# Spectra operands made four products ahead, stored spectra requested by ScalarE, another order of units

## The chip, the cores and the metric

The kernel runs on one core of one Trainium2 chip. A core has five engines with queues of their own: TensorE (matmuls; PE in the rows, its weight loads PEld), VectorE (DVE), ScalarE (ACT), GpSimd (POOL) and SyncE (SP), which here only requests transfers. Sixteen DMA engines move data between the main memory and the on-chip memory; requests to them come from the queues of SyncE, GpSimd and ScalarE. The metric is the device time in microseconds of one execution. Before the change it is 2862.4 us, the median of three runs (2861.56 to 2863.65).

## The reference, cut to what matters

The reference computes two layers of a diffusion backbone over 1024 latent tokens and 256 context tokens of width 1024. The change touches the first layer alone, and there the Hyena half of the mixer: two long convolutions, each with a filter that a small network makes, applied in the frequency domain.

```python
def long_conv(u, filt, skip):
    L = u.shape[1]
    uf = jnp.fft.rfft(u, n=2 * L, axis=1)
    ff = jnp.fft.rfft(filt, n=2 * L, axis=0)
    y = jnp.fft.irfft(uf * ff[None], n=2 * L, axis=1)[:, :L]
    return y + u * skip

def hyena_mix(p, conv_w, conv_b, w1, b1, freq, w2, b2, w3, skip):
    ...
    v = x1 * long_conv(v, filt[:, 0], skip[0])
    v = x2 * long_conv(v, filt[:, 1], skip[1])
    return v.astype(p.dtype)
```

Around it stand the input projection, a Fourier mixer on the other half of the channels, the output projection, a gated feed-forward block, and a second layer with neighbourhood attention.

## The kernel before, in words

All products run in fp32r, an fp32 format of reduced precision. Each operand is therefore split into a high part, rounded by ScalarE (line 350), and a low part, the difference, subtracted by VectorE (line 352). A product is then three matmuls: high by high, high by low, low by high. All matmuls of the transforms are written by one helper (line 346), all requests of SyncE by another (line 331, `ld`), those of ScalarE by a third (`lda`, line 334) and those of GpSimd by a fourth (`ldr`, line 337), so that rows of the profile show these lines.

The Fourier transforms are matmuls with stored cosine and sine matrices, folded by symmetry. A frequency belongs to a class: even or odd index (`cls` 0 or 1), and cosine or sine (`eo`).

**Spectra of the filters.** `spectrum_l(o, ...)` makes the spectrum of the filter of convolution `o` (0 or 1) for the latent tokens while the input projection runs; both are woven together by generators, in a list that says how many steps of the filter work follow each block of the projection. For each class in the order 2, 3, 0, 1 it takes four operands, each a sum or difference of filter rows in a high and a low part, with a stored matrix: sixteen operands in all. Two operands (`k` = 0, 1) share a group of twelve matmuls, into two accumulators (`f` = 0, 1). The inner generator `operands()` makes them: it loads a pair of matrices (`cast2`, two `tk` tiles out of a pool of four, requested by GpSimd, which rounds while it moves), forms the sums on VectorE (`sums`, lines 958 to 975, and lines 998 to 1002), and splits them. For class 0 it first forms `f0` (lines 982 to 984), and the first group of that class also makes the highest frequency, with products whose output has two rows (128*2 in the rows). The list `ready` holds the operands that are made before they are used; each product takes one out and asks for another. The spectra are stored in main memory by SyncE, a pair of 128 by 512 blocks for each class and block of frequencies.

**The units.** After the projection, `unit(o, fb, cls)` computes one block `fb` of 128 frequencies of class `cls` of the transformed input, and multiplies it with the stored spectrum. It requests its matrices (16 bit, rounded by ScalarE at lines 399 and 414; or through GpSimd, where `wide` is set), requests the stored spectrum `F` (an `s4` tile of 128 by 1024, 512 KB, from a pool of 21), and runs its matmuls in two halves: a class 0 unit has 6 matmuls in each half, a class 1 unit 12. The first half needs the input rows of even index, the second those of odd index. Then `combine_l` forms the complex product: two wide VectorE multiplications (lines 1256 and 1257), two additions on GpSimd (line 1261 and the next), and, one unit later, the split in `parts()` (ScalarE line 1273, VectorE line 1275). The split result keeps two `s4` tiles until the inverse has used it. Eight units make a convolution, so sixteen of the 21 tiles then hold results.

**Between the two convolutions.** `inverse_first` computes the inverse of the first convolution and the gate `x1`, in two passes `j` = 0, 1; each pass gives half of the rows that the second convolution transforms (even ones in the first pass). In the last pass it starts the first halves of four units of the second convolution, so that TensorE has work while VectorE makes the odd rows; the fourth of them uses the two `pq` accumulators, the others the six `ps` ones. Afterwards each unit is finished and the unit four places later started. `inverse_last` (line 1425) follows, with the Fourier mixer of the latent tokens woven in.

**What sets the order.** The program text gives each instruction a priority by its place. A planner, part of the framework, then plays the program through with costs of its own, and fixes for each engine an order, by what is ready and has a free buffer in its play, earliest in the text first. On the chip each queue keeps that order. So a generator step that is taken earlier raises the priority of its instructions, and a load waits for its buffer at the head of the queue that requests it.

Of the kernel before, what the change touches and what calls it, by code (L numbers as in the profile page):

```python
# [258 lines left out]
class Builder:  # L259
# [685 lines left out]
    def spectrum_l(self, o, raw, tot):  # L945
# [32 lines left out]
        def operands():  # L978
            for i in classes:
                if i == 0:  # L980
                    f0 = self.f0 = self.S2()
                    V.tensor_copy(f0, fe)
                    V.tensor_tensor(f0[0:1, :], fe[0:1, :], fo[0:1, :], ADD)
                    V.scalar_tensor_tensor(f0[0:1, :], f0[0:1, :], 0.5, self.taps0[o][0:1, :], op0=MUL, op1=ADD)
                even = []
                for p in (0, 1):
                    with self.follow(self.row_ld):
                        mt = self.cast2(a["ff_l"][i, p])
                    for k in (0, 1):
                        if i % 2 == 0:  # L990
                            if p == 0:
                                even.append(sums(i, k))
                            t = even[k][p]
                        else:
                            f, r = (raw[(p + 2 * k, q, i // 2)] for q in (0, 1))
                            t = self.T()
                            if i == 1 and p + k == 0:
                                V.scalar_tensor_tensor(t, r, m1, f0, op0=MUL, op1=ADD)
                            elif p + k == 0:
                                V.scalar_tensor_tensor(t, f, m0, r, op0=MUL, op1=ADD)  # L1000
                            else:
                                V.tensor_tensor(t, f, r, SUB if i == 1 else ADD)
                        xh, xl = self.S2(F32R), self.S2(F32R)
                        self.split(t, xh, xl)
                        yield xh, xl, mt[k]

        ops = operands()
        ready = [next(ops), next(ops)]
        yield
        for i in classes:  # L1010
            cls, eo = i % 2, i // 2
            kept = []
            for p in (0, 1):
# [22 lines left out]
                for f in (0, 1):  # L1036
                    fb = 2 * p + f
                    if eo:
                        self.frg[("l", o, cls, fb)] = self.DR([2, P, HC])
                    d = self.frg[("l", o, cls, fb)]  # L1040
# [276 lines left out]
    def unit(self, o, fb, cls, bank=None, wide=False):  # L1317

        a = self.a
        tr = self.tr  # L1320
        if cls == 0:
            src = a["vfe_l"][fb]
            mt = self.cast4(src) if wide else self.cast(1024, src) if o + fb == 0 else self.cmat(1024, src)
            mats = [mt[:, :512], mt[:, 512:]]
            q = 2 * (fb // 2)
            xs = [range(q, q + 2), range(4 + q, 6 + q)]
        else:
            src = a["vfo_l"][fb]
            half = [src[:, j * 1024:j * 1024 + 1024] for j in (0, 1)]
            mats = [self.cast4(x) for x in half] if wide else [self.cast(1024, x) for x in half] if o + fb == 0 else self.cmat2(src)  # L1330
            xs = [range(4, 8), range(4)]
        F = self.S4()
        d = self.frg[("l", o, cls, fb)]
        self.ld(F.rearrange("p (e c) -> p e c", e=2), d[0:2].rearrange("e p c -> p e c"))
        row = None
        if cls == 0 and fb == 0:
            row = self.TK()
            self.ld(row[0:1, :], self.frow[("l", o)])
        bank = bank or self.PS
        spec = [bank(), bank()]  # L1340
        n = len(xs[0])
        H = n * P
        for half in (0, 1):
            for ps, mt, x in zip(spec, mats, xs):
                for b in range(half, n, 2):
                    sl, sk = slice(b * P, (b + 1) * P), slice(H + b * P, H + (b + 1) * P)
                    xh, xl = tr[x[b]]
                    self.mm(ps, mt[:, sl], xh, b == 0, False)
                    self.mm(ps, mt[:, sl], xl, False, False)
                    self.mm(ps, mt[:, sk], xh, False, b == n - 1)  # L1350
            yield
        self.combine_l(o, cls, fb, spec, F, row)
        yield
# [1177 lines left out]
    def run(self):  # L2531
# [78 lines left out]
        for k, (fb, cls) in enumerate(((0, 1), (0, 0), (1, 1), (1, 0), (2, 1), (3, 1), (2, 0), (3, 0))):  # L2610
# [5 lines left out]
            if k in (0, 1, 6):  # L2616
                next(cc)
        self.parts()
        units = [self.unit(1, fb, cls, self.PQ if k % 4 == 3 else None, k in (2, 3))
                 for k, (fb, cls) in enumerate(((0, 1), (1, 1), (2, 1), (0, 0), (1, 0), (3, 1), (2, 0), (3, 0)))]  # L2620
        for _ in range(2):
            next(cc)
        for _ in self.inverse_first(units[:4]):
# [136 lines left out]
        for i, _ in enumerate(first_part(1)):  # L2760
            if i == 7:
                c = self.rms_begin(0)
# [54 lines left out]
        c = self.rms_begin(1)  # L2817
# [87 lines left out]
```

## Time and profile before

| | before |
|---|---|
| median of three runs | 2862.4 us |
| profiled execution, its own time | 2867.56 us |
| its span, first to last instruction | 2865.8 us |
| TensorE busy | 2779.7 us, 97% |
| VectorE busy | 2045.2 us, 71% |
| ScalarE busy | 1321.0 us, 46% |
| GpSimd busy | 543.2 us, 19% |
| mean granted clock of TensorE | 0.984 |

The rows in the prediction come from these views. The page gives the totals. The stretches give for each interval its length, then the busy time and number of instructions of TensorE, its weight loads, VectorE, ScalarE and GpSimd, then the clock that TensorE was granted (1.00 is full), the share of the DMA engines in use, and their rate in GB/s. The timeline gives start, duration, engine, line, operation, output and inputs by tile name, shapes and a count; in brackets stands how long the engine was idle before it, and what released it. The waits give engine, line and what was waited for, with the total, the number of times and the longest, in microseconds. Times are counted from the start of the span. Tile names are cut of their numbers: `s` is any tile of the `s2` and `s4` pools, `ps` and `pq` are accumulators, `d` is main memory.

### The profile page before, as it was taken

To read this page: it belongs to the slowest core of one execution; us is meant where nothing else is said; L and a number is where in the kernel's file an instruction comes from. 1 tells how busy PE (TensorE), PEld (TensorE's weight loads), DVE (VectorE), ACT (ScalarE), POOL (GpSimd) and SP (SyncE) were. 2 spreads that over 40 slices of the span, in tenths; PEclk is the share of its full clock that TensorE was granted. 3 is DMA by queue.
4 is the path that set the end of the run, shared out by engine and by line. 5 is a ranking of instruction groups with operands and counts; after the bars stand their busy time and mean duration, and the time that the engine had idled before them with its cause. 6 is when DMAs were issued, how large, how long until landed. Compare 5 with 4: busy or idle time off the path is not lost.

```text
span 2865.8 us, 43630 instructions
## 1 busy us (share of the span) xinstructions
PE 2779.7 (97%) x15610; PEld 2325.6 (81%) x15610; DVE 2045.2 (71%) x3531; ACT 1321.0 (46%) x2269; POOL 543.2 (19%) x880
## 2 busy tenths in 40 slices
PE   7999999999999999999999999999999999999998
PEld 4876678788899888888888888888887788888887
DVE  6766777768777888866777536878867987655556
ACT  5433335443554333333455326888755533333434
POOL 2210234241001211222110002332212122112000
PEclk9999899999999999999999999999999999999999
DMA  7356525655556656658884436777856366434763
GB/s 267 120 167 214 158 83 190 220 172 219 204 189 210 207 192 200 212 196 328 308 308 154 147 120 143 195 203 200 227 199 215 122 242 224 144 110 167 234 195 133
DMA packets 296887, 554.21 MB, mean 193 GB/s; under 512 B 81872, under 2 KB 128658, under 8 KB 296670
## 3 DMA queue, kind: packets, MB, share of 16 engines
q1 hardware_dynamic: 232318, 361.06, 40.0%
q0 software_dynamic: 61504, 185.65, 18.6%
q10 hardware_dynamic: 2848, 4.72, 0.4%
q8 instruction: 123, 2.02, 0.3%
q14 instruction: 94, 0.77, 0.1%
HBM read 405.01 MB, written 118.76 MB: 183 GB/s over the span
## 4 chain that ended last, share of the span: by engine, by line
PE 71%; issue 3%; DVE 3%; DMA 2%; ACT 1%; POOL 1%; DVEq 0%; SPq 0%; POOLq 0%; ACTq 0%
PE ps L1932 25%; PE ps L346 15%; PE ps L2109 11%; PE pq L346 9%; PE pq L1932 3%; PE pq L2109 3%; PE ps L2230 2%; PE ps L2463 1%; PE ps L1425 1%; DMA s<-d 1%; DMA s<-in_c_ctx 1%; DMA g<-in_bias 0%; DMA s<-in_x_t 0%; DVE wl L352 0%; DVE s L352 0%
## 5 line engine op out<-in xcount | busy, mean ns | idle before, releaser
L1932 PE MATMUL ps<-s,s 128*128 128x512 f32 x2012 | 498.6, 391 | 3.3 <-DVE s L1823 1.7
L1932 PEld LDWEIGHTS ps<-s,s 128*128 128x128 f32 x2012 | 379.4, 189 | 83.9 <-DVE s L1823 2.6
L346 PE MATMUL ps<-s,wh 128*128 128x256 f32 (+1 forms) x1776 | 403.3, 331 | 6.0 <-ACT wh L350 2.5
L346 PEld LDWEIGHTS ps<-s,wh 128*128 128x128 f32 x1776 | 296.3, 191 | 41.3 <-ACT wh L350 3.4
L346 PE MATMUL ps<-s,wl 128*128 128x256 f32 (+1 forms) x888 | 267.1, 329 | 0.1
L2109 PE MATMUL ps<-s,s 128*128 128x512 f32 (+1 forms) x1000 | 259.7, 383 | 3.2 <-DVE s L352 3.1
L350 ACT CAST s<-s 128x1024 fp32r<-128x1024 f32 (+2 forms) x192 | 173.0, 926 | 192.0 <-DMA s<-d 172.3
L346 PE MATMUL pq<-s,wh 128*128 128x512 f32 (+1 forms) x848 | 260.9, 389 | 0.3 <-ACT wh L350 0.3
L352 DVE TENSOR_TENSOR wl<-ws,wh 128x1024 fp32r<-128x1024 f32 (+1 forms) x141 | 168.2, 1194 | 118.4 <-ACT wh L350 113.9
L350 ACT CAST wh<-ws 128x1024 fp32r<-128x1024 f32 (+1 forms) x141 | 144.7, 1026 | 204.4 <-PE ps L346 85.4
L346 PE MATMUL ps<-s,s 128*128 128x65 f16 (+4 forms) x2748 | 230.3, 235 | 6.3 <-DVE st L2446 2.6
L352 DVE TENSOR_TENSOR s<-s,s 128x1024 fp32r<-128x1024 f32 (+2 forms) x170 | 191.0, 1154 | 58.3 <-ACT s L350 58.2
L352 DVE TENSOR_TENSOR s<-t,s 128x512 fp32r<-128x512 f32 (+2 forms) x238 | 151.5, 652 | 104.6 <-ACT s L350 81.7
L350 ACT CAST s<-t 128x512 fp32r<-128x512 f32 (+2 forms) x238 | 133.8, 582 | 188.4 <-PE ps L1932 68.0
L2109 PEld LDWEIGHTS ps<-s,s 128*128 128x128 f32 x1000 | 184.4, 188 | 41.2 <-DVE s L352 4.8
L1932 PE MATMUL ps<-s,wh 128*128 128x512 f32 x624 | 194.8, 390 | 0.0
L346 PEld LDWEIGHTS ps<-s,wl 128*128 128x128 f32 x888 | 165.6, 190 | 16.6 <-DVE wl L352 0.6
L337 POOL DMA_DIRECT2D d<-s x186 | 101.4, 546 | 376.5 <-DVE s L1739 92.9
L346 PEld LDWEIGHTS pq<-s,wh 128*128 128x128 f32 x848 | 150.5, 189 | 22.8 <-issue 1.2
L346 PE MATMUL pq<-s,wl 128*128 128x512 f32 (+1 forms) x424 | 161.8, 382 | 1.3 <-DVE wl L352 1.3
L2109 PE MATMUL ps<-s 128*128 128x512 f32 (+1 forms) x500 | 150.7, 385 | 0.0
L346 PEld LDWEIGHTS ps<-s,s 128*128 128x128 f32 (+1 forms) x828 | 129.3, 192 | 22.3 <-issue 4.4
(487 smaller groups left out, 5485.8 us busy)
## 6 DMA issues: line engine op xcount, KB each, us to landing
s<-d SPq DMA_DIRECT2D x282, 256.0 KB, 3.9
d<-s POOLq DMA_DIRECT2D x170, 256.0 KB, 3.7
s<-in_down SPq DMA_DIRECT2D x150, 256.0 KB, 4.1
s<-in_ada_w POOLq DMA_DIRECT2D x64, 512.0 KB, 5.0
ws<-in_up SPq DMA_DIRECT2D x44, 512.0 KB, 3.7
d<-g POOLq DMA_DIRECT2D x86, 256.0 KB, 3.1
ws<-in_gate SPq DMA_DIRECT2D x42, 512.0 KB, 4.3
d<-tk POOLq DMA_DIRECT2D x66, 256.0 KB, 4.0
```

The costliest lines, as they stand in the source:

```text
L337: self.last_ldr = self.nc.gpsimd.dma_start(out, in_).ins
L346: self.last_mm = self.nc.tensor.matmul(o, l, r, start=st, stop=sp).ins
L350: self.last_hi = nc.scalar.copy(hi, src).ins
L352: self.last_lo = eng.tensor_tensor(lo, src, hi.bitcast(F32), SUB).ins
L1425: nc.tensor.matmul(d, s, w, start=cb not in first, stop=e == 1 and i == 1 and f == 3 and k == 2, skip_group_check=True)
L1932: nc.tensor.matmul(ps, x[:, sl], y, start=first and j == 0 and x is wh and y is xh, stop=j == 3 and x is wl, skip_group_check=True)
L2109: m = nc.tensor.matmul(acc[j][:, c0:c1], x[:, sl], y[:, xs], start=first and k == 0, stop=last and k == 2, skip_group_check=True)
L2230: m = nc.tensor.matmul(o, x[:, nb * P:(nb + 1) * P], t[:, c:c + 256], start=kb == 0 and k == 0 and nb % 2 == 0, stop=kb == NFB - 1 and k = ...
L2463: nc.tensor.transpose(ps[:, j * P:(j + 1) * P], src[:, j * P:(j + 1) * P], self.ident)
```

## The change: what it does

It has three parts, at three places.

1. In `spectrum_l`, four operands are made before the first product, where there were two; since each product takes one and asks for one, the generator stays four ahead.
2. In `unit`, the stored spectrum `F` is requested by ScalarE, where SyncE did it. This holds for the sixteen units of both convolutions.
3. In `run`, the units of the second convolution stand in another order. The flags that go with the place stay: the third and fourth unit take their matrices through GpSimd, the fourth and eighth use the `pq` accumulators.

```diff
@@ spectrum_l
         ops = operands()
-        ready = [next(ops), next(ops)]
+        ready = [next(ops) for _ in range(4)]
         yield
@@ unit
         F = self.S4()
         d = self.frg[("l", o, cls, fb)]
-        self.ld(F.rearrange("p (e c) -> p e c", e=2), d[0:2].rearrange("e p c -> p e c"))
+        self.lda(F.rearrange("p (e c) -> p e c", e=2), d[0:2].rearrange("e p c -> p e c"))
         row = None
@@ run
         units = [self.unit(1, fb, cls, self.PQ if k % 4 == 3 else None, k in (2, 3))
-                 for k, (fb, cls) in enumerate(((0, 1), (1, 1), (2, 1), (0, 0), (1, 0), (3, 1), (2, 0), (3, 0)))]
+                 for k, (fb, cls) in enumerate(((0, 0), (0, 1), (1, 0), (1, 1), (2, 1), (3, 1), (2, 0), (3, 0)))]
```

## The prediction

> **What bounds the kernel now.** I read the page first, then the waits of TensorE, then the stretches around its longest waits, and last the order on VectorE, ScalarE and the queues there.
>
> ```profile
> span 2865.8 us, 43630 instructions
> PE 2779.7 (97%) x15610; PEld 2325.6 (81%) x15610; DVE 2045.2 (71%) x3531; ACT 1321.0 (46%) x2269; POOL 543.2 (19%) x880
> PE 71%; issue 3%; DVE 3%; DMA 2%; ACT 1%; POOL 1%; DVEq 0%; SPq 0%; POOLq 0%; ACTq 0%
> ```
>
> TensorE is busy for 97% of the span and carries 71% of the chain of waits. It has 86 us without work (2865.8 − 2779.7), and the change can gain only from its gaps, and from what follows a gap. Four gaps lie where the diff works: two in the stored spectra (about 177 and 297 us), one where the inverse of the first convolution starts (510), one behind the units of the second convolution (568). These are the stretches (length, busy time of each engine with counts, granted clock, share and rate of the DMA engines):
>
> ```profile
> 177.00:193.00 16.00, 13.02 (x33) 7.57 (x32) 8.15 (x15) 2.53 (x5) 0.99 (x2) 0.68 0.41 133
> 297.00:318.00 21.00, 16.43 (x43) 9.92 (x42) 12.30 (x20) 7.46 (x13) 2.34 (x5) 0.67 0.61 199
> 510.30:522.00 11.70, 8.18 (x25) 6.54 (x25) 3.49 (x8) 2.69 (x4) 2.30 (x5) 0.71 0.94 316
> 568.00:590.00 22.00, 17.65 (x97) 14.86 (x97) 18.69 (x17) 9.56 (x11) 19.52 (x13) 0.84 0.39 129
> ```
>
> In each the idle time is only a part of the loss: behind the gap the granted clock is low, 0.67 to 0.84 over the stretch. The same twelve products show it, before the second gap and after it:
>
> ```profile
> 282.96 3.01 PE L346 MATMUL ps<-s,tk 128*128 128x512 f32 x12
> 310.32 5.07 PE L346 MATMUL ps<-s,tk 128*128 128x512 f32 x12
> ```
>
> So I count as lost the idle time plus length times (1 − clock): 2.98 + 5.12 = 8.1 us; 4.57 + 6.93 = 11.5; 3.52 + 3.39 = 6.9; 4.35 + 3.52 = 7.9. That is 34 us in all, and it is the most that the change can bring; where idle time and low clock overlap it is a little less.
>
> **Part 1, four operands ahead in the spectra.** Sixteen operand pairs are made per order, in the classes 2, 3, 0, 1; the gaps stand at the first products of class 0.
>
> ```profile
> 166.82 2.88 PE L346 MATMUL pq<-s,tk 128*128 128x512 f32 x12
> 172.03 0.62 PE L346 MATMUL ps<-s,tk 128*128 128x512 f32 x2
> 180.30 0.40 PE L346 MATMUL ps<-s,c 128*2 128x512 f32 x1 [2.66 <-ACT s L350]
> 288.68 0.63 PE L346 MATMUL pq<-s,tk 128*128 128x512 f32 x2
> 301.99 0.58 PE L346 MATMUL ps<-s,c 128*2 128x512 f32 x1 [3.44 <-ACT s L350]
> ```
>
> TensorE waits there for ScalarE's rounding (line 350), which waits for VectorE, and VectorE is late for one reason: the class 0 operands take seventeen instructions of it, and it began them late.
>
> ```profile
> 167.70 1.30 DVE L352 TENSOR_TENSOR s<-t,s 128x512 fp32r<-128x512 f32 x2 [7.23 <-ACT s L350]
> 168.91 0.48 DVE L982 COPY s<-s 128x512 f32<-128x512 f32 x1
> 180.28 0.69 DVE L352 TENSOR_TENSOR s<-t,s 128x512 fp32r<-128x512 f32 x1
> 283.22 1.29 DVE L352 TENSOR_TENSOR s<-t,s 128x512 fp32r<-128x512 f32 x2 [2.57 <-ACT s L350]
> 284.43 0.42 DVE L982 COPY s<-s 128x512 f32<-128x512 f32 x1
> 301.97 0.69 DVE L352 TENSOR_TENSOR s<-t,s 128x512 fp32r<-128x512 f32 x1
> ```
>
> From the copy at 168.91 to the last subtraction at 180.28 VectorE is busy without a break, some 12 us, after it had stood idle for 7.23 us. The operands are asked for two products earlier under the change. Two products are one group of twelve matmuls: class 3's first group starts at 166.82 and its second at 172.03, so the request moves up by 5.2 us in the first order; in the second order the groups start at 282.96 and 288.68, 5.7 us. Both leads are larger than the waits (2.66 and 3.44), and VectorE has room before (7.23 and 2.57 idle). If the planner keeps the order in which the work is written, both waits close and the low clock behind them goes too: 8.1 + 11.5 = 19.6 us.
>
> What is late next are the stored matrices. A pair of them takes two of the four `tk` buffers, so four operands ahead fill all four, and the loads of the next pair wait for the release whatever the program asks for.
>
> ```profile
> 308.27 0.53 POOL L337 DMA_DIRECT2D tk<-in_ff_l  x1 [11.05 <-PE ps L346]
> tk<-in_ff_l POOLq DMA_DIRECT2D x32, 256.0 KB, 3.2
> 317.54 1.63 PE L346 MATMUL ps<-s,tk 128*128 128x512 f32 x6 [0.79 <-DMA tk<-in_ff_l]
> ```
>
> A load is there 0.53 + 3.2 = 3.7 us after its buffer is free, while the other pair keeps TensorE busy for about 2.7 us (twelve starts within the 3.01 quoted). Where nothing else is on TensorE, that is 1.0 us of waiting per pair, for the two pairs of class 1 in both orders: 4 us given back. The 17 VectorE instructions now compete with the evacuations of the input projection that they used to follow; no row shows that competition, and I bound it by 0 and by the gap that it would reopen, 2.66 us an order, and take 1.3 each, as the idle 7.23 us is nearer to no competition at all. Part 1: 19.6 − 4 − 2.6 = **13 us**; ends 0 and 19.6. Two more pairs of `s2` buffers are held, of 35; no row tells how many are free.
>
> **Part 2, the stored spectra requested by ScalarE.** Sixteen loads of 512 KB leave SyncE's queue.
>
> ```profile
> 502.37 1.23 DVE L1256 TENSOR_TENSOR s<-ps,s 128x1024 f32<-128x1024 f32 x1 [2.90 <-DMA s<-d]
> L1256 DVE TENSOR_TENSOR s<-ps,s 128x1024 f32<-128x1024 f32 x14 | 17.0, 1217 | 12.8 <-DMA s<-d 7.7 <-PE ps L346 5.1
> SPq L331 <- ACT mat L414: 53.7, 11, 13.0
> L334 ACTq DMA_DIRECT2D d<-s x16: 326/326/1144, 1371.8 to 1529.3; - x16
> 450.00:500.00 50.00, 49.22 (x256) 41.65 (x257) 41.15 (x50) 33.18 (x50) 30.04 (x20) 1.00 0.61 201
> ```
>
> Today SyncE stands for 53.7 us behind matrices whose buffers ScalarE still reads, and VectorE waits 7.7 us in all for the spectra queued behind them. The last of these, 2.90 us, is ahead of the third gap. A request of ScalarE took 0.326 us, so sixteen are 5.2 us of its sequencer, and in the 50 us of the first units ScalarE is busy for 33.18 only. TensorE, though, is busy for 49.22 of these 50: what VectorE gains there is hidden, and only the third gap can pay.
>
> ```profile
> 510.78 0.67 DVE L1384 TENSOR_TENSOR t<-tk,ps 128x512 f32<-128x512 f32 x1
> 512.58 1.21 DVE L1275 TENSOR_TENSOR s<-s,s 128x1024 fp32r<-128x1024 f32 x1
> 513.85 22.91 PE L346 MATMUL ps<-s,mat 128*128 128x512 f32 x88 [3.52 <-DVE s L1275]
> ```
>
> The subtraction that ends this gap stands on VectorE behind line 1384, which reads what TensorE itself has just finished. An earlier spectrum moves it only if the planner also puts it ahead of that line. Between 0 and 6.9 us I take **1**, nearer to the row. The Trainium skill (DMA: Bandwidth & Descriptors, Issuing engines are not separate DMA queues) says that requesting from several engines saves only sequencer time, usually small beside the transfer; by it this part would be 0 and the sum 1 us smaller. The trace shows the request itself late, by SyncE's 53.7 us of standing, which the page does not weigh.
>
> **Part 3, the order of the second convolution's units.** The work is the same: four units of 12 matmuls (class 0), four of 24 (class 1), and the same loads. The old first unit is a 24.
>
> ```profile
> 547.21 0.74 PE L346 MATMUL ps<-s,mat 128*128 128x512 f32 x2 [0.94 <-ACT s L350]
> 558.14 11.21 PE L346 MATMUL ps<-s,mat 128*128 128x512 f32 x48 [0.81 <-ACT mat L399]
> 575.56 0.74 PE L1425 MATMUL ps<-mat,s 128*128 128x256 f32 x4 [2.34 <-DVE s L1257]
> 550.64 0.68 DVE L352 TENSOR_TENSOR s<-g,s 128x512 fp32r<-128x512 f32 x1
> 556.46 1.23 DVE L1256 TENSOR_TENSOR s<-ps,s 128x1024 f32<-128x1024 f32 x1 [5.13 <-PE ps L346]
> ```
>
> VectorE ends the transformed rows at 551.3 and then waits 5.13 us for a first finished unit; later TensorE waits for VectorE's combinations (2.34 us and smaller ones, the fourth stretch). With (0, 0) first, a unit needs six matmuls behind rows that are made first of all, so VectorE starts about 5 us earlier, and the combinations behind it with it: 5.0 of the 7.9 us lost. Against it, the first halves started ahead are 6 + 12 + 6 + 12 = 36 matmuls in place of 42; 6 at 0.23 us (11.21 us for 48) uncover 1.4 us near 547, where 0.94 us is open already. Part 3: **3.6 us**; ends −1.4 and 7.9.
>
> The sum is 13 + 1 + 3.6 = 17.6 us. The profiled execution took 2867.56 us with its span of 2865.8; the median shown is 2862.4, 5.2 us lower, and the gaps have no reason to differ, so I take the sum from the median: 2844.8, **2845 us**, own range 2835 to 2852.
>
> **Rivals.** *The matrices take the place.* The waits at class 0 go, but the loads into four `tk` buffers become the rhythm, and each 1.0 us wait brings the low clock back for a group (5.07 − 3.01 = 2.06 us): two pairs in two orders, 4 × 3.06 = 12.2 us given back of 19.6. With part 3 alone beside it the gain is 7.4 + 3.6 = 11: 2851 us. For it speaks the 0.79 us already open; against it, that matmuls of the input projection fill such places elsewhere. The Trainium skill (TensorE: Matmul & The Clock Gate, The HAM clock gate) puts the drop to half rate behind at least one idle window of about 3.4 us; by it waits of 1.0 us would leave the clock alone and this rival would shrink into the forecast. The trace shows a lower clock after a wait of 2.66 us already (0.68 in the first stretch).
>
> *The order does not move.* The operands need `t` buffers (six here) and `s2` buffers as well; if these are what the planner waits for, the class 0 chain begins where it began, part 1 is nothing, and part 3 alone leaves 2859 us. For it speaks that ScalarE's and VectorE's order comes out of the planner, not out of the text; against it, VectorE's 7.23 idle us with ScalarE as releaser, not a buffer.
>
> *ScalarE is held by its requests: slower.* A request waits, in ScalarE's own queue, for a free `s4` buffer; the stored products hold sixteen of 21. Behind it stand the roundings of matrices and products that TensorE needs. ScalarE has 16.8 idle us for the eight requests of the first units (50 − 33.18), 2.1 us each: that is the point from which TensorE pays. At a mean hold of 3.6 us it pays 1.5 × 16 = 24 us, more than the 17.6 gained: 2869 us. For it speaks the tight buffer; against it, that the planner places the request where its model has the buffer free, and that today's requests mostly found their buffer free at once.
>
> **How the numbers follow.** Forecast 0.48, matrices 0.22, order unmoved 0.15, ScalarE held 0.15. About 0.2% (5.7 us) is what can be told from no change. The first two are faster by more, 0.70; the third lies within it, 0.15; the last is slower, 0.15. The range is 2832 (the 34 us nearly whole) to 2868, which takes in the first three and the near end of the fourth.
>
> **What would show it.** Part 1 right: no wait at the 128*2 products of class 0, a granted clock near 1.00 from 177 to 193 and from 297 to 318, class 0's copy (line 982) some 5 us before its place today. Wrong: the same waits, or waits for `tk` loads. Part 2: no VectorE wait for spectra between 457 and 504, and the third gap about as long as now; wrong if ScalarE idles ahead of roundings with a request in its queue. Part 3: VectorE's first combination within 2 us of the last row, and waits below 2 us behind the units. The forecast is wrong as a whole if gaps of this size with their low clock open elsewhere, since a shifted plan can move any later instruction.

## The result, and the profile after

The changed kernel takes 2852.68 us, the median of seven runs (2849.41 to 2857.97), beside 2862.40 us for seven runs of the kernel before (2857.96 to 2864.04). The ratio is 0.9967, 95% interval 0.9956 to 0.9978: 9.4 us gained, with an interval of 6 to 13 us. A later comparison gave 0.9967 again (0.9955 to 0.9978). The forecast was 2845 us, a gain of 17.6.

The profiled execution after took 2850.3 us, 17.3 less than the one before (2867.56). That is nearly twice what the medians differ by: the one before lies 5.2 us above its median, the one after 2.4 below. So a stretch of these two traces may be read for what happens in it, but the gain is read from the medians.

The page of the kernel after, its totals and the DMA queue of ScalarE's requests:

```profile
span 2848.5 us, 43624 instructions
PE 2762.6 (97%) x15610; PEld 2314.2 (81%) x15610; DVE 2044.6 (72%) x3531; ACT 1319.0 (46%) x2269; POOL 543.9 (19%) x880
q10 hardware_dynamic: 7200, 13.11, 1.4%
```

The last line is part 2 at work: that queue moved 13.11 MB, where it moved 4.72 before, and the difference is sixteen spectra of 512 KB.

The first thing to see is where the gain is not. TensorE was idle for 86.1 us before (2865.8 − 2779.7) and is idle for 85.9 us now (2848.5 − 2762.6). The same 15610 matmuls took 17.1 us less busy time. What the change brought is granted clock, not idle time removed.

Every timed run comes with the span and the mean granted clock, so this can be taken over runs. Span times (1 − clock) is an estimate of the time lost to a lowered clock; the rest of the span holds the work at full clock and all idle time. In the two traces it is 45.9 and 28.5 us, 17.4 apart, close to the 17.1 us of busy time. Means, with the standard error of the two parts:

| kernel | runs | span | lost to the clock | the rest |
|---|---|---|---|---|
| before | 79 | 2859.8 | 37.5 (0.5) | 2822.3 (0.3) |
| after | 12 | 2850.5 | 28.0 (0.9) | 2822.4 (0.9) |

The spans differ by 9.3 us; the loss to the clock by 9.5, the rest by nothing.

The stretches show the place. First the kernel before, from the first product of the filter spectra to the last one, then the kernel after, the same work, and two shorter stretches of it (columns as in the prediction):

```profile
143.40:323.20 179.80, 167.84 (x739) 118.88 (x740) 113.11 (x204) 57.64 (x100) 19.62 (x37) 0.91 0.57 187
```

```profile
144.40:314.90 170.50, 158.54 (x748) 114.35 (x749) 113.45 (x204) 56.64 (x100) 19.72 (x37) 0.98 0.61 199
177.00:193.00 16.00, 15.77 (x73) 11.26 (x73) 9.12 (x16) 5.09 (x9) 2.64 (x5) 1.00 0.60 188
297.00:318.00 21.00, 18.54 (x88) 13.88 (x87) 5.09 (x8) 5.40 (x9) 6.04 (x12) 1.00 0.61 180
```

The stretch is 9.3 us shorter. Its idle time is 11.96 us in both (179.80 − 167.84; 170.50 − 158.54). Its clock rose from 0.91 to 0.98: lost time 16.2 us before, 3.4 us after, 12.8 less. That it is not shorter by as much is because nine more matmuls of the projection lie in it (748 against 739), some 2 us, and because the clock is given to a hundredth, 1.8 us of such a stretch. The two places where the prediction saw the gaps, 177 to 193 and 297 to 318, now run at full clock.

The waits did not vanish, they moved. The timeline of the kernel after, TensorE:

```profile
279.42 0.96 PE L346 MATMUL pq<-s,tk 128*128 128x512 f32 x3 [0.45 <-DMA tk<-in_ff_l]
280.79 0.97 PE L346 MATMUL pq<-s,tk 128*128 128x512 f32 x3 [0.40 <-DMA tk<-in_ff_l]
284.96 0.64 PE L346 MATMUL ps<-s,wh 128*128 128x256 f32 x2 [3.21 <-ACT s L1043]
294.65 1.64 PE L346 MATMUL ps<-s,c 128*2 128x512 f32 x6
307.43 1.65 PE L346 MATMUL pq<-s,tk 128*128 128x512 f32 x6 [0.67 <-ACT s L1043]
309.42 1.65 PE L346 MATMUL ps<-s,tk 128*128 128x512 f32 x6 [0.34 <-DMA tk<-in_ff_l]
316.78 0.73 PE L346 MATMUL ps<-s,wh 128*128 128x512 f32 x2 [1.45 <-DVE s L1053]
504.16 1.22 PE L346 MATMUL ps<-s,mat 128*128 128x512 f32 x2 [3.55 <-DVE s L1275]
536.19 0.73 PE L346 MATMUL ps<-s,mat 128*128 128x512 f32 x2 [2.30 <-ACT s L350]
562.71 0.52 PE L1425 MATMUL ps<-mat,s 128*128 128x256 f32 x3
595.07 0.47 PE L346 MATMUL pq<-mat,s 128*128 128x256 f32 x2 [1.05 <-DVE t L1240]
```

The class 0 products with two output rows (128*2) start with no wait, where they waited 3.44 us. In place of that wait stands one of 3.21 us ten microseconds ahead of them: a matmul of the input projection waits for an accumulator, which ScalarE has not yet copied away (line 1043). With the smaller ones of the second order the new waits are 6.5 us (0.45 + 0.40 + 3.21 + 0.67 + 0.34 + 1.45); the three that the prediction showed of the spectra were 6.9 (2.66 + 3.44 + 0.79). ScalarE and VectorE of the kernel after show why:

```profile
283.81 0.62 ACT L350 CAST s<-t 128x512 fp32r<-128x512 f32 x1 [3.65 <-DVE t L970]
284.33 1.06 ACT L1043 COPY s<-ps 128x512 f32<-128x512 f32 x2
```

```profile
162.04 0.40 DVE L982 COPY s<-s 128x512 f32<-128x512 f32 x1
273.14 0.42 DVE L982 COPY s<-s 128x512 f32<-128x512 f32 x1
501.69 0.68 DVE L1385 TENSOR_TENSOR t<-tk,ps 128x512 f32<-128x512 f32 x1
502.29 0.68 DVE L1511 TENSOR_TENSOR s<-t 128x128 f32<-128x128 f32 x3
502.89 1.21 DVE L1275 TENSOR_TENSOR s<-s,s 128x1024 fp32r<-128x1024 f32 x1
539.62 0.68 DVE L352 TENSOR_TENSOR s<-g,s 128x512 fp32r<-128x512 f32 x1
540.22 1.22 DVE L1256 TENSOR_TENSOR s<-ps,s 128x1024 f32<-128x1024 f32 x1
590.07 0.69 DVE L1240 TENSOR_TENSOR t<-pq,tk 128x512 f32<-128x512 f32 x1 [4.32 <-DMA tk<-d]
593.63 0.69 DVE L1241 TENSOR_TENSOR t<-pq,tk 128x512 f32<-128x512 f32 x1 [2.88 <-DMA tk<-d]
```

The class 0 chain begins earlier, at 162.04 in place of 168.91 and at 273.14 in place of 284.43. Of the 11.3 us of the second order, 4.6 are what the first had already saved (the matmul at 216.90 before stands at 212.26). ScalarE stands idle for 3.65 us ahead of the chain's rounding (line 350 at 283.81), which waits for the sum of line 970, and the copy of line 1043 stands behind it in the same queue.

The third gap is as it was: 3.55 us, 3.52 before, and line 1275 stands behind lines 1385 and 1511 in VectorE's order. Behind the units, VectorE combines its first unit at 540.22, directly behind the last row (539.62), and line 1425 starts without a wait, where it waited 2.34 us. The wait near the end of the inverse grew from 0.94 to 2.30 us.

One more view of the kernel after, the groups, on part 2:

```profile
L1256 DVE TENSOR_TENSOR s<-ps,s 128x1024 f32<-128x1024 f32 x14 | 17.0, 1217 | 7.9 <-DMA s<-d 6.9 <-PE ps L346 1.0
```

VectorE still waits 6.9 us for stored spectra (7.7 before). SyncE, without their requests in its queue, stands behind the matrices of line 414 no less than before: 72.5 us over the whole span, 67.0 before. (The 53.7 us in the prediction are those between 430 and 600 us alone.)

### The profile page after: what moved, and what is told of

It is laid out like the page before. It is cut to its first block, busy times and chain, and to the rows that moved or that the text cites. A ratio compares the mean times of both kernels' runs of the same rounds, so it can differ in the third digit from the quotient of the medians.

```text
span 2848.5 us, 43624 instructions
## 1 busy us (share of the span) xinstructions
PE 2762.6 (97%) x15610; PEld 2314.2 (81%) x15610; DVE 2044.6 (72%) x3531; ACT 1319.0 (46%) x2269; POOL 543.9 (19%) x880
## 3 DMA queue, kind: packets, MB, share of 16 engines
q10 hardware_dynamic: 7200, 13.11, 1.4%
```

## The experiments: the parts alone

**Part 1 alone.** The kernel before with

```diff
-        ready = [next(ops), next(ops)]
+        ready = [next(ops) for _ in range(4)]
```

> Part 1 alone (four operands ahead; requests and unit order as before). Theory A (the gain comes from part 1 in the spectra and from part 3 behind the units, part 2 gives nothing): ratio 0.9978, 6 us under the kernel before; no wait at the 128*2 products of class 0, one wait of about 3 us in the second order for an accumulator that ScalarE's line 1043 reads; the gaps where the inverse starts (3.5 us) and behind the units (some 4 us) as before. Rival B (the gain is mostly from part 3 and from later stages): ratio above 0.999.

Measured: 2856.87 us, ratio 0.9986 (0.9976 to 0.9995), a gain of 4.0 us with an interval of 1.4 to 6.9. In its trace the spectra take 170.8 us (144.6 to 315.4), as in the whole change:

```profile
144.60:315.40 170.80, 157.02 (x748) 114.08 (x749) 113.45 (x204) 56.64 (x100) 19.71 (x37) 0.99 0.61 199
```

So part 1 takes 9.0 us out of its own stretch, by the clock (0.99), and the time shows 1.4 to 6.9 of it. Over the runs of this kernel the loss to the clock is 30.4 us (1.2), 7.1 less than before, and the rest of the span is 2824.7 us (0.9), 2.4 more. Where those 2.4 us lie, one trace doesn't tell: the stretch behind the spectra, up to the first unit, is 129.7 us here and 129.3 before, and the remainder of the span behind line 1425 scatters from one trace to another by more, from 2211.4 us (parts 1 and 3) to 2221.5 (part 2 alone).

**Part 2 alone.** The kernel before with

```diff
-        self.ld(F.rearrange("p (e c) -> p e c", e=2), d[0:2].rearrange("e p c -> p e c"))
+        self.lda(F.rearrange("p (e c) -> p e c", e=2), d[0:2].rearrange("e p c -> p e c"))
```

> Part 2 alone (stored spectra requested by ScalarE). Theory A: no difference, ratio 1.000 within 0.001; VectorE still waits 2 to 3 us for the spectra of three units of the first convolution, and the gap where the inverse starts stays at 3.5 us. Rival C (ScalarE is held by its requests and part 2 costs what the other two bring beyond the measured gain): ratio 1.002 or more, 6 us slower, with ScalarE idle ahead of roundings.

Measured: 2863.6 us, ratio 1.001 (0.9996 to 1.0024). Not told from no change. The groups of its trace:

```profile
L1256 DVE TENSOR_TENSOR s<-ps,s 128x1024 f32<-128x1024 f32 x14 | 17.0, 1217 | 14.4 <-DMA s<-d 9.3 <-PE ps L346 5.1
```

VectorE waits longer for the spectra, 9.3 us in place of 7.7. Taking the request out of SyncE's queue did not make it early. One of these requests in the timeline, first the kernel before, then this one:

```profile
485.38 0.38 SPq L331 DMA_DIRECT2D s<-d  x1
```

```profile
485.34 0.37 ACTq L334 DMA_DIRECT2D s<-d  x1
```

The seven between 460 and 498 us came at 460.49, 468.73, 475.93, 479.92, 485.38, 488.68 and 496.83 from SyncE, and at 460.00, 467.01, 475.62, 479.71, 485.34, 490.32 and 497.12 from ScalarE. So what holds a request back is not the queue that it stands in.

**Part 3 alone.** The kernel before with

```diff
-                 for k, (fb, cls) in enumerate(((0, 1), (1, 1), (2, 1), (0, 0), (1, 0), (3, 1), (2, 0), (3, 0)))]
+                 for k, (fb, cls) in enumerate(((0, 0), (0, 1), (1, 0), (1, 1), (2, 1), (3, 1), (2, 0), (3, 0)))]
```

> Part 3 alone (the other order of the second convolution's units). Theory A: ratio 0.9988, 3.5 us faster: the waits of TensorE behind the units (2.34 us and smaller, with the low clock behind them) go, the wait near the end of the first inverse grows from 0.94 to about 2.3 us. Rival B: ratio 0.998 or less.

Measured: 2861.53 us, ratio 1.0001 (0.9992 to 1.0009): nothing. In its trace the stretch from the first unit product to line 1425 is 119.5 us (123.1 before), 3.6 us shorter. The stretch of line 1425 behind it is 75.4 us (71.3 before), 4.1 us longer. Its timeline, TensorE, VectorE and SyncE, and the stretch around the waits:

```profile
609.91 0.77 PE L346 MATMUL pq<-mat,s 128*128 128x256 f32 x2 [3.94 <-DVE t L1240]
```

```profile
608.48 0.69 DVE L1241 TENSOR_TENSOR t<-pq,tk 128x512 f32<-128x512 f32 x1 [5.41 <-DMA tk<-d]
```

```profile
599.21 0.38 SPq L331 DMA_DIRECT2D tk<-d  x1
```

```profile
605.00:625.00 20.00, 15.48 (x81) 13.19 (x80) 9.62 (x16) 8.09 (x12) 3.73 (x4) 0.83 0.39 135
```

The units end earlier, but the stored spectra of the context hardly come earlier: SyncE requested the last of them at 599.21, 2.6 us earlier than before (601.78), and it landed 9.2 us later. The kernel before had no wait for them. The gain is spent in waiting, and the clock is 0.83 over the stretch around the wait.

**Parts 1 and 3, without part 2.** Both diffs of these on the kernel before.

> Parts 1 and 3 without part 2. Theory A: as the whole change, ratio 0.9967, 9.4 us faster than before. Rival C (part 2 costs): ratio 0.995 or less, 14 us faster. Rival D (part 2 brings a part of the gain): 0.998 or more.

Measured: 2851.45 us, ratio 0.9972 (0.9960 to 0.9983). That is the whole change, 1.2 us from it at the medians and well within its interval: part 2 adds nothing that can be told. By the ratio it gains 8.0 us (4.9 to 11.4), the two parts alone 4.0 and −0.3; the 4.3 us by which it is more are about what three such intervals leave open. VectorE's timeline:

```profile
591.93 0.69 DVE L1240 TENSOR_TENSOR t<-pq,tk 128x512 f32<-128x512 f32 x1 [3.34 <-DMA tk<-d]
594.65 0.69 DVE L1241 TENSOR_TENSOR t<-pq,tk 128x512 f32<-128x512 f32 x1 [2.03 <-DMA tk<-d]
```

VectorE waits for the context's spectra as long as with part 3 alone (3.34 + 2.03 us, 5.41 there), but TensorE doesn't wait for line 1240 in this trace, and the stretch of line 1425 takes 68.9 us, where part 3 alone had 75.4. In these two traces, then, part 3's gain is kept with part 1 and spent without it. Why TensorE is not held beside part 1 was not tried.

## The experiments: the waits that took the place

All of these are edits of the kernel after.

**The third gap.** Ahead of line 1275 VectorE runs a step of the context's convolution (lines 1508 to 1511). It is moved behind the last unit.

```diff
-            if k in (0, 1, 6):
+            if k in (0, 1):
...
-        for _ in range(2):
+        for _ in range(3):
```

> The changed kernel, with the last step of the context tokens' first convolution (lines 1508 to 1511 on VectorE) taken after the last unit of the latent tokens, where it stood one unit earlier. Theory E (the gap where the inverse starts is a matter of VectorE's order, not of late spectra): the subtraction of line 1275 that ends the gap runs as soon as ScalarE's rounding is there, about 3 us earlier, the gap of 3.55 us falls below 1 us and its low clock (3.4 us at half) goes; 4 to 5 us under the changed kernel, ratio near 0.995. Rival F (the last spectrum is the cause): the gap stays above 2.5 us, ratio 0.9967.

Measured: 2851.46 us, ratio 0.9971 (0.9960 to 0.9982). The timeline:

```profile
495.20 3.27 PE L346 MATMUL ps<-s,mat 128*128 128x512 f32 x7 [2.54 <-ACT mat L399]
507.35 3.02 PE L346 MATMUL ps<-s,mat 128*128 128x512 f32 x12 [0.27 <-DVE s L1275]
```

The gap closed, from 3.55 to 0.27 us, with the spectra requested by the same queue: VectorE's order is what ends it. In the kernel after, line 1275 ran 3.2 us after ScalarE's rounding was ready, behind line 1384; here it runs 1.0 us after it, and ahead of line 1384. (VectorE's wait for the last spectrum is shorter here too, 0.72 us in place of 2.70. In the kernel after, line 1384 began 0.5 us after TensorE had stopped, so with that order an earlier spectrum could have brought no more than that.) The time is the same as that of the kernel after (2851.46 against 2852.68, intervals alike). Twelve microseconds earlier TensorE now waits 2.54 us for a matrix that ScalarE rounds, and behind the units it waits 4.79 us for line 1240, where it waited 1.05.

**Three ahead in place of four.**

```diff
-        ready = [next(ops) for _ in range(4)]
+        ready = [next(ops) for _ in range(3)]
```

> The changed kernel with three operands ahead in place of four. Theory G (the new wait of 3.2 us in the second order is that of the accumulators of class 3's first group, whose copies of line 1043 stand on ScalarE behind both class 0 roundings): with three ahead only one of these roundings is in front, the wait falls under 1 us, while the lead of one product (2.6 to 2.9 us) still covers the old waits nearly whole; 1 to 4 us under the changed kernel. Rival H (the lead is what counts): the old waits at the 128*2 products come back with 1 us or more, and the time is 2 us or more above the changed kernel.

Measured: 2849.67 us, ratio 0.9948 (0.9931 to 0.9964), the lowest so far. The timeline:

```profile
281.59 0.98 PE L346 MATMUL pq<-s,tk 128*128 128x512 f32 x3 [0.76 <-DMA tk<-in_ff_l]
283.71 1.34 PE L346 MATMUL pq<-s,tk 128*128 128x512 f32 x3 [1.14 <-DMA tk<-in_ff_l]
286.24 0.80 PE L346 MATMUL ps<-s,wh 128*128 128x256 f32 x2 [1.19 <-ACT s L1043]
```

The wait for the accumulator fell from 3.21 to 1.19 us. Of the waits at class 0, that of the second order did not come back, and that of the first came back with 0.69 us (2.66 before the change). The waits for stored matrices grew from 0.85 us (0.45 + 0.40) to 1.90.

**One more buffer for the spectra.** An `s4` tile more, paid with two `s2` tiles.

```diff
-        self.p4 = ent(tc.tile_pool(name="p4", bufs=21))
-        self.p2 = ent(tc.tile_pool(name="p2", bufs=35))
+        self.p4 = ent(tc.tile_pool(name="p4", bufs=22))
+        self.p2 = ent(tc.tile_pool(name="p2", bufs=33))
```

> The changed kernel with 22 tiles of 128 by 1024 in place of 21, and 33 of 128 by 512 in place of 35. Theory I (the spectra are requested late since they wait for a tile in the planner's play, whichever engine requests them): VectorE's three waits of 2.1 to 2.7 us for spectra fall below 1 us each, the time within 3 us of the changed kernel. Rival J (they stand in ScalarE's order): the waits stay above 1.5 us each.

Measured: 2871.22 us, ratio 1.0028 (1.0015 to 1.0041): slower than before the change. The groups:

```profile
L1256 DVE TENSOR_TENSOR s<-ps,s 128x1024 f32<-128x1024 f32 x14 | 17.1, 1218 | 6.9 <-PE ps L346 3.7 <-DMA s<-d 3.2
```

The waits for spectra fell from 6.9 to 3.2 us: with one more buffer they are less late, where another queue made no difference. The third gap shrank with it, from 3.55 to 0.61 us, though the work ahead of line 1275 was not moved by hand; the plan is another one with another pool, and has line 1275 ahead of line 1384. So the buffer as the cause is the likely reading, and not shown apart from the plan. What it cost stands in the stages behind. The stretch from the end of line 1425 to the end of the attention, first this kernel, then the kernel after:

```profile
639.60:2138.20 1498.60, 1474.99 (x9447) 1272.45 (x9447) 1101.15 (x2030) 757.76 (x1372) 271.49 (x481) 1.00 0.65 207
```

```profile
634.50:2122.10 1487.60, 1472.40 (x9448) 1273.58 (x9447) 1112.60 (x2030) 758.68 (x1372) 270.47 (x481) 1.00 0.66 208
```

The same matmuls take 11 us more, 8.4 of them idle time (23.6 against 15.2). That the two `s2` tiles are missed there is likely; no run shows it by itself. Theory I had the time within 3 us of the kernel after, and missed this.

**The context's spectra requested by ScalarE**, for the waits of 4.32 and 2.88 us behind the units.

```diff
-        self.ld(fr, d[0])
-        self.ld(g, d[1])
+        self.lda(fr, d[0])
+        self.lda(g, d[1])
```

> The changed kernel with the stored spectra of the context tokens requested by ScalarE as well. Theory K (with the units done earlier, these spectra, queued on SyncE behind matrices, are what comes late next): VectorE's waits for them at lines 1240 and 1241 (4.3 and 2.9 us) fall below 1 us, TensorE's wait of 1.0 us behind them goes; up to 2 us under the changed kernel, ratio 0.996 to 0.9967. Rival L (the transfers themselves are late, whoever asks): the waits stay.

Measured: 2861.72 us, ratio 1.0003 (0.9990 to 1.0015): the whole gain of the change is lost. VectorE's timeline:

```profile
596.62 0.69 DVE L1240 TENSOR_TENSOR t<-pq,tk 128x512 f32<-128x512 f32 x1 [7.42 <-DMA tk<-d]
598.75 0.69 DVE L1241 TENSOR_TENSOR t<-pq,tk 128x512 f32<-128x512 f32 x1 [1.43 <-DMA tk<-d]
```

The waits are 8.85 us in all, where they were 7.20, as Rival L had it. Its reason, late transfers, is not the whole: ScalarE requests the two only at 590.24, where SyncE in the kernel after did at 583.03 and 585.83, and from request to use it is some 6 to 8 us in both. The loss of 9 us in the time is more than these 1.65 us. Over the runs the loss to the clock is 5.4 us above that of the kernel after, and the rest of the span 4.7; where they arise was not followed further.

## The experiments: is three better than four?

**The kernel after once more**, unaltered.

> The changed kernel once more, unaltered, to stand beside the three kernels of this call. Theory M (three operands ahead are better than four): this kernel keeps its first ratio, 0.9967 within 0.001, and the kernel with three ahead is 2 us or more below it. Theory N (the lead of three ahead in the earlier comparison, 3.0 us, was scatter): the two are within 1.5 us of each other.

Measured: 2851.64 us, ratio 0.9967 (0.9955 to 0.9978).

**Three ahead once more**, the kernel of above.

> The whole change with three operands made ahead in place of four, once more. Theory M: ratio 0.994 to 0.9958, since the wait for an accumulator ahead of class 0 of the second order fell from 3.21 us to 1.19 us and the old waits at class 0 stayed away. Theory N: 0.996 to 0.9975, the same as four ahead, since the two waits for stored matrices (0.76 and 1.14 us) that stood in the trace of three ahead take back what the accumulator gave.

Measured: 2848.52 us, ratio 0.9955 (0.9943 to 0.9967). It is 3.1 us below the kernel after on the same chip, and 0.9955 lies within what Theory M gave. Over all runs the mean spans are 2846.3 us for ten runs of it and 2850.5 for twelve of the kernel after, each with a standard error of some 0.7, so 4.2 us apart with an interval of 2 to 6. Three ahead beat four, and this kernel is the fastest of the study, though within one comparison the intervals of the two ratios overlap. The waits account for a part of it: TensorE's waits between 279 and 287 are 4.06 us with four (0.45 + 0.40 + 3.21, in the trace shown) and 3.09 and 3.51 us in the two traces with three, one of 1.45 us behind the last class (for line 1053) falls to 0.26 us, and against these 0.69 and 0.68 us came back at class 0 of the first order. Over the runs, 2.4 of the 4.2 us are loss to the clock (28.0 against 25.6), and 1.8 the rest of the span.

**Three ahead without part 2.** The kernel of above with the spectra requested by SyncE.

```diff
-        self.lda(F.rearrange("p (e c) -> p e c", e=2), d[0:2].rearrange("e p c -> p e c"))
+        self.ld(F.rearrange("p (e c) -> p e c", e=2), d[0:2].rearrange("e p c -> p e c"))
```

> Three operands ahead and the other order of units, with the stored spectra still requested by SyncE. Theory P (who requests the spectra is worth nothing): within 2 us of the kernel with three ahead and the whole change. Rival Q (with three ahead the third gap begins to pay): slower than that kernel by 3 us or more, and VectorE's waits for spectra, 7.7 us before the change, are back.

Measured: 2853.3 us, ratio 0.9973 (0.9961 to 0.9984), 4.8 us above three ahead with part 2. The time is what Rival Q said, its reason is not there: VectorE's waits for spectra are 7.4 us, 7.5 us in the trace with part 2, and the third gap is 3.56 and 3.55 us. Theory P is wrong too. With four ahead the same step changed nothing that can be told (2851.45 against 2852.68 us). The difference stands in the loss to the clock, 30.7 us (1.4) against 25.6 (1.0), with the rest of the span equal (2820.9 and 2820.7). What sets the clock off in the one and not in the other stays open.

**Three ahead and the third gap closed**, both edits together.

> Three operands ahead, and the step of the context's convolution that VectorE did ahead of the third gap moved behind the last unit. Theory R (the gains of separate places add up where no new wait opens): the 3.55 us wait behind line 1275 falls under 1 us, and the time is 2 to 4 us below three ahead alone, ratio near 0.9935. Rival S (that gain goes into a wait for a matrix of ScalarE ahead of it, 2.54 us when it was tried with four ahead): within 1.5 us of three ahead alone.

Measured: 2850.83 us, ratio 0.9968 (0.9957 to 0.9979), 2.3 us above three ahead alone. The timeline:

```profile
487.71 11.91 PE L346 MATMUL ps<-s,mat 128*128 128x512 f32 x44 [2.30 <-ACT mat L399]
499.91 23.87 PE L346 MATMUL ps<-s,mat 128*128 128x512 f32 x104 [0.28 <-DVE s L1275]
592.91 0.47 PE L346 MATMUL pq<-mat,s 128*128 128x256 f32 x2 [3.44 <-DVE t L1240]
```

As Rival S had it, the gap of 3.55 us became a wait of 2.30 us for a matrix; and a wait behind the context's spectra, 3.44 us where it was 0.73, stands behind the units. So the time is further up than the 1.5 us that Rival S allowed.

## Why the prediction was right in its direction and too large

*What bounds the kernel.* The reading held: gains come from what follows a gap. It held more strictly than the prediction used it. I counted idle time and low clock together as recoverable, 34 us. The idle time of the four stretches turned up elsewhere, and only low clock was recovered: 86.1 and 85.9 us of idle time.

*Part 1, the sum of 13 us, was the term that was mis-sized.* Its direction and its first step were right: the class 0 chain began 6.9 and 11.3 us earlier, more than the 5 us predicted, no wait stands at the 128*2 products, the clock there is 1.00. So the order does move, and that rival falls. Of the 19.6 us the stretch gave 8.6 to 9.3 (170.5 to 171.2 us in three traces with four ahead, 179.8 before), and the time 4.0 by itself. The two things set against it were these. The stored matrices were put at 4 us and cost 1.2 (0.45 + 0.40 + 0.34 us, the last at 309). "They compete with the evacuations of the input projection" was put at 2.6 us for two orders, and looked for on VectorE. It came on ScalarE, as one wait of 3.21 us in the second order, with a lowered clock behind it (0.88 from 282 to 296). This is the step that failed. I had no row for it and took the middle of two bounds, and the upper bound left out the clock: a gap that opens again costs its idle time and what the clock loses behind it, not 2.66 us alone. Of the 10.3 us missing in the stretch, that wait and its clock are 4.9 (3.21 and 14 × 0.12), the matrices 1.2, the waits at 307 and 317 for line 1043 and line 1053 are 2.1, and some 2 are the nine matmuls more, which are no loss. What is missing between the stretch and the whole time, 9.0 against 4.0 us, is the larger part of the error, and stays open. The matrices did not take the place in the sense of the rival: its time, 2851 us, is the nearest to the measured one, but by luck, for its waits of 1.0 us were 0.34 to 0.45.

*Part 2, 1 us, measured nothing* (1.001, 0.9996 to 1.0024). The reason given for the small price, that VectorE's order and not the spectrum ends the third gap, is shown by the run that moved that work: 3.55 to 0.27 us. The condition put beside it, that the line must also be put ahead of line 1384, was met in that run and in the one with one more `s4` tile (0.61 us). The reason given for any price at all was wrong. SyncE's standing was not what made the spectra late: without them in its queue they are requested at nearly the same times and are as late as before (6.9 us, and 9.3 with part 2 alone), and with one more buffer they are less late (3.2 us). The Trainium skill (DMA: Bandwidth & Descriptors, Issuing engines are not separate DMA queues) gave this part as 0; part 2 alone and the runs with four ahead agree with it (1.001, and 2851.45 against 2852.68 us). With three ahead the kernel was 4.8 us faster with part 2 than without, for a reason that stays open. ScalarE was not held: the rival at 2869 us falls.

*Part 3, 3.6 us.* Each of its two numbers is in the trace: the wait at line 1425 went (2.34 to none), and the uncovered 1.4 us came at the inverse (0.94 to 2.30, 1.36 us). Its stretch is 3.6 us shorter, with some luck in the exact figure: in the trace of part 2 alone, without this part, the stretch is 2.3 us shorter than before (120.8), at a clock of 1.00 in place of 0.97. The idle time in it is 6.1 us with part 3 alone and 8.5 before. What the prediction did not ask is what is late next: the context's spectra, which take back all of it where part 3 stands alone.

*The sum.* It was made of terms that were to add up. The parts alone gave 4.0, −2.9 and −0.3 us, the last two not told from nothing; together they gave 9.4. The traces show one way in which they hang together, TensorE's wait behind the context's spectra, which eats part 3's gain alone (3.94 us) and not beside part 1; whether that is the whole of the difference stays open, as does the gap between the 9.0 us that part 1 takes out of its stretch and the 4.0 us of its time.

*The one-execution caution* was right: the sum was taken from the median, not from the profiled 2867.56 us, and the traces alone would have shown 17.3 us.

## What to carry to other kernels

Where an engine is busy for 97% of the span, a change of order can leave its idle time as it was and still gain, because a gap is paid twice, by its length and by the clock behind it; look at both before and after. Ask of every stall that is removed which in-order queue its work now stands in, and what that queue held up before: here the operands' rounding went ahead of a copy on ScalarE that freed an accumulator. How far ahead is a number to be tried in steps: with three in place of four that copy was less late (1.19 and 1.66 us in place of 3.21), and of the old waits only 0.69 us came back.

## What the runs showed that was not expected

The clock does not answer a given wait in a given way. The same kernel, three ahead, twice over the same stretch of the program, first in the one trace and then in the other:

```profile
282.00:296.00 14.00, 11.67 (x50) 9.60 (x49) 13.98 (x25) 6.15 (x11) 0.00 (x0) 0.76 0.31 102
```

```profile
282.00:296.00 14.00, 11.96 (x63) 9.23 (x61) 14.00 (x26) 6.64 (x11) 1.06 (x2) 1.00 0.28 81
```

The waits in it and just ahead of it are 0.76, 1.14 and 1.19 us in the first and 1.47, 0.38 and 1.66 us in the second, 3.09 and 3.51 us in all. The first lost a quarter of its clock for 14 us, the second nothing. The kernel before is as scattered, 2851.49 to 2870.94 us over twenty runs on one chip. In the traces the clock falls to one half for 3.4, 6.8, 10.2 or 13.7 us at a time, and in each of the fourteen traces all its falls and rises lie on one grid of 3.41 us. Two windows of that grid, first in the one trace and then in the other:

```profile
280.61:284.03 3.42, 1.52 (x6) 0.79 (x6) 3.42 (x6) 0.62 (x1) 0.90 (x2) 1.00 1.09 360
284.03:287.44 3.41, 2.22 (x8) 1.50 (x7) 3.41 (x7) 2.35 (x5) 0.00 (x0) 0.50 0.25 67
```

```profile
280.28:283.69 3.41, 1.90 (x6) 0.97 (x6) 3.41 (x6) 0.62 (x1) 0.36 (x1) 1.00 1.11 360
283.69:287.10 3.41, 1.88 (x15) 1.88 (x16) 3.41 (x7) 3.03 (x6) 0.00 (x0) 1.00 0.03 7
```

In the first trace TensorE is idle for 1.90 us of one window, 56% of it, and the next has half the clock. In the second the waits are spread over two windows, 44% and 45% idle, and the clock stays. The other windows of the fourteen traces bear this out (100 us at either end of the span left out; the ends of matmuls are modelled, so the shares are rough). Of 115 windows at full clock in which TensorE was idle for half or more, 108 were followed by one at half clock; of 61 with 40 to 50%, 15; of 10479 with less, 19. Of the windows at half clock, all 39 with 20% idle time or more were followed by another such window, and 16 of 151 with less than 10%.

The Trainium skill (TensorE: Matmul & The Clock Gate, The HAM clock gate) says that activity is watched in windows of about 3.4 us that run freely, whatever the kernel does, and that the clock halves after at least one idle window. The lengths in steps of 3.4 us and the two traces above agree with windows that run freely. That a whole window must be idle does not agree: the two waits ahead of the fall in the first trace are 0.76 and 1.14 us, and before the change 2.66 us was enough. By the counts above half a window is mostly enough, and short waits within one window add up. For a forecast it means that what a gap of some 1.7 to 3.4 us costs in clock is a chance, not a number: it depends on where the grid falls.
